# The FFN's second product with its last twelve feature blocks as a seven-product Strassen block product

## The chip, the cores and the metric

The kernel runs on one core of one Trainium2 chip. The metric is the time of the whole kernel in device microseconds (us); the median of three runs stands for a version. One more execution was taken by the hardware profiler, and all rows below come from it. Engines carry the profile's names: PE (matmul), PEld (weight load of the matmul engine), DVE (vector), ACT (scalar), POOL (GpSimd), SP (the engine that issues most transfers).

## The reference

One layer of a streaming encoder on x of 512 tokens by 1024 channels, in float32. Attention branches come first and make an intermediate x. Then the feed-forward part (FFN), of which the last product concerns us:

```python
h = rmsnorm(x, g_ffn_pre[l])
gu = h @ w_ffn_in[l]
f = (jax.nn.silu(gu[..., :D_FF]) * gu[..., D_FF:]) @ w_ffn_out[l]
x = x + rmsnorm(f, g_ffn_post[l])
```

D_FF is 2816, that is 22 feature blocks of 128; `w_ffn_out` is 2816 by 1024. So the product is 512 tokens by 2816 features by 1024 channels.

## The kernel before

Every float32 operand of a matmul is split into a high part (rounded by ACT, line 74) and a low part (the rest, subtracted by DVE, line 75), and every product is made of three matmuls: high by high, high by low, low by high. So a feature block of the second product, for one 128-token tile and one half of the channels (512 columns), is three matmuls with a 128 by 128 stationary side and 512 moving columns.

The first FFN product (`blocks`, `seven`, `left_sides`) is already a Strassen product of seven products per feature block. It leaves the gated result of feature block j in `fT[j]`, features on the partitions and 512 tokens in the columns; two neighbouring blocks share a buffer of the tag `act`.

The second product is `tok_pair` (lines 731 to 764), called with all four token tiles and `tail=4`. Its first 18 feature blocks run block by block: load the 128 by 1024 block of weights (SP, 512 KB), split it, split `fT[k]` (class `Parts`), and then for each of four token tiles six matmuls at line 745, which alternate between the two banks of that tile, 24 in all. The last four blocks (`tail`) run tile by tile and bank by bank, 24 matmuls to a tile, three in a row into one bank; when a tile is done, `done` calls `post_norm` (line 767) for it while PE goes on with the next tile. Four tiles by two halves fill all eight PSUM banks.

`post_norm` squares both halves with a sum (ACT, line 231), makes the reciprocal root (DVE line 240, POOL line 241, DVE lines 246 and 247), multiplies by the gain row (DVE, line 774), adds the residual (DVE, line 779) and stores two halves (line 781; SP and ACT queues).

Buffers: loads alternate between the tags `wraw` (3 buffers) and `lraw` (2). The split weights of alternate blocks go to `wh` and `wl` (2 each) or to `w2` (4 buffers that hold both parts). `act` has 22 buffers, `h` 8, `gate` (the scratch of `post_norm`) 2.

The order on PE is the order in which the program is written. On the other engines a planner fixes an order when the program is built: among instructions that it thinks ready it takes the one written first. On the chip each engine then runs its list in that order, and an instruction that waits holds all behind it.

Of the kernel before, what the change touches and what calls it, by code (L numbers as in the profile page):

```python
# [11 lines left out]
F32 = mybir.dt.float32  # L12
F32R = mybir.dt.float32r
AF = mybir.ActivationFunctionType
OP = mybir.AluOpType
AX = mybir.AxisListType

P = 128
T = 512
D = 1024  # L20
NK = D // P
NT = T // P
DFF = 2816
NF = DFF // P
# [23 lines left out]
class Layer:  # L48
# [41 lines left out]
    def load(self, src, kc, c, tag=None):  # L90

        self.nw += 1
        tag = tag or ("lraw" if self.late and self.nw % 2 else "wraw")
        raw = self.big(tag, F32)[:, :kc * c]
        self.nc.sync.dma_start(raw.rearrange("p (k c) -> p k c", c=c), src.rearrange("(k p) c -> p k c", p=P))
        return raw, c
# [164 lines left out]
    def run(self):  # L261
        w_in, w_kv = self.a["w_in"], self.a["w_mem_kv"]
        late = ExitStack()
        att = ExitStack()
        self.att = att.enter_context(self.tc.tile_pool(name="att", bufs=1))
        with self.tc.manual_schedule(engines={mybir.EngineType.PE}):
            self.setup()
            memT, mk, mv, cq = [], {}, {}, {}
            self.index_keys(cq)
            xs = [self.load_rows(self.a["mem"], t) for t in range(2)]  # L270
            for x in xs:
                self.norm_in(x)

            self.iq = {}
            iqs = lambda js: self.feat_tiles(w_in[:, C_IQ:C_IQ + 512], self.hT, self.iq, js, T - P, P,
                                             lambda ps: self.evac_q(ps[:, 0:T - P], T - P), self.w_iq)
            cqs = lambda js: self.feat_tiles(w_in[:, C_CQ:C_CQ + 512], self.hT, cq, js)
            mks = lambda js: self.feat_tiles(w_kv[:, 0:512], memT, mk, js, n=M)
            mvs = self.tok_tiles(w_kv[:, 512:1024], memT, (0, 1), mv)
            memTs = self.mem_T(xs, memT)  # L280
            iq = self.add(iqs(range(4)))
            kv = self.add(cqs((1,)), self.mix(memTs, cqs((2,)), 2), mks(range(4)), cqs((3,)), mvs)
            self.drain(iq)
            self.scores()
            self.drain(kv)
            a, aq = self.qkv(C_AQ, C_AK, C_AV)
            self.branch_c(cq, mk, mv)
            self.acc = {}
            self.add(self.merge(2, self.outC, "w_up_c"))
            self.drain(aq)  # L290
            self.select()
            self.fill(FM)
            b, bq = self.qkv(C_BQ, C_BK, C_BV)
            self.branch_a(*a)
            self.drain(bq)
            self.add(self.merge(0, self.outA, "w_up_a"))
            self.outB = []
            self.add(self.merge(1, self.outB, "w_up_b"))
            self.branch_b(*b)
            self.drain()  # L300
            att.close()
            self.late = late.enter_context(self.tc.tile_pool(name="late", bufs=1))
            self.mix_out()
            self.ffn()
        late.close()
# [625 lines left out]

    def ffn(self):
        nc, a = self.nc, self.a
        w_out = a["w_ffn_out"]
        fT = []

        def out(j):
            if j % 2 == 0:
                self.slot = self.big("act", F32)
            fT.append(self.slot[:, (j % 2) * T:(j % 2 + 1) * T])  # L940
            return fT[j]

        def products(pss, ws, t):
            c = slice(256 * t, 256 * t + 256)
            for ps, w in zip(pss, ws):
                yield from self.feat(ps[:, c], w, self.h2, t0=256 * t, n=256)

        run = lambda g: [None for _ in g]
        first = []
        for j, w in enumerate(self.first_ffn):  # L950
            u = (self.bank(), self.bank()), w
            run(products(*u, 0))
            first.append(u)
        pss, ws = first[0]
        for k in range(NK + 2):
            if k < NK:
                next(self.last_h2)
            if k > 1:
                for ps, w in zip(pss, ws):
                    self.feat_k(ps[:, 256:512], w, self.h2, k - 2, n=256, t0=256)  # L960
        self.gated(pss, out(0))
        y = self.right_sides()
        for j, u in enumerate(first[1:], 1):
            run(products(*u, 1))
            self.gated(u[0], out(j))
        self.blocks(range(self.NFIRST, NF), y, out)
        gp = self.grow("g_ffn_post", "h")

        def done(t, ps):
            self.post_norm(ps, gp, self.x1[t], a["out"][t * P:(t + 1) * P, :])  # L970

        self.done = done
        pairs = {}

        class Parts:
            def __getitem__(_, k):
                if k not in pairs:
                    pairs[k] = self.pair("act")
                    self.split(*pairs[k], fT[k])
                return pairs[k]  # L980

        run(self.tok_pair(w_out, Parts(), NF, range(NT), tail=4))


# [16 lines left out]
```

## Time and profile before

| what | value |
|---|---|
| median of 3 runs | 912.36 us (912.33 to 912.51) |
| the profiled execution, as a run | 910.88 us |
| its span, first to last instruction | 909.1 us |
| mean granted TensorE clock | 0.998 of full speed |
| PE busy | 888.3 us, 98% of the span |
| DVE, ACT, POOL busy | 641.5, 458.6, 117.1 us |

The busy time of an engine is the sum over all stages; what limits a stage is read from that stage's own window. A matmul's row shows its whole passage (about 0.39 us for 512 columns), of which neighbours overlap, so the pace is read from the distance between starts.

### The profile page before, as it was taken

To read this page: it belongs to the slowest core of one execution; us is meant where nothing else is said; L and a number is where in the kernel's file an instruction comes from. 1 tells how busy PE (TensorE), PEld (TensorE's weight loads), DVE (VectorE), ACT (ScalarE), POOL (GpSimd) and SP (SyncE) were. 2 spreads that over 40 slices of the span, in tenths; PEclk is the share of its full clock that TensorE was granted. 3 is DMA by queue.
4 is the path that set the end of the run, shared out by engine and by line. 5 is a ranking of instruction groups with operands and counts; after the bars stand their busy time and mean duration, and the time that the engine had idled before them with its cause. 6 is when DMAs were issued, how large, how long until landed. Compare 5 with 4: busy or idle time off the path is not lost.

```text
span 909.1 us, 13518 instructions
## 1 busy us (share of the span) xinstructions
PE 888.3 (98%) x5146; PEld 780.1 (86%) x5146; DVE 641.5 (71%) x1120; ACT 458.6 (50%) x808; POOL 117.1 (13%) x153
## 2 busy tenths in 40 slices
PE   8999999999999999999999999899999999999997
PEld 7888888888888888888788888899999999888885
DVE  6589999953688976787563478788888887932215
ACT  6465674332666665666353355455555555811111
POOL 2000000020132304433212123400000000000000
PEclk9999999999999999999999999999999999999999
DMA  6523543454354433222483624213333334533002
GB/s 203 173 83 117 168 111 93 127 128 116 104 156 112 128 82 92 70 59 58 140 252 107 185 83 127 71 47 95 115 109 102 114 97 139 164 97 106 29 1 92
DMA packets 129541, 101.17 MB, mean 111 GB/s; under 512 B 4652, under 2 KB 115292, under 8 KB 129476
## 3 DMA queue, kind: packets, MB, share of 16 engines
q1 hardware_dynamic: 128884, 99.26, 37.9%
q10 hardware_dynamic: 592, 1.05, 0.3%
q8 instruction: 40, 0.66, 0.3%
q14 instruction: 25, 0.20, 0.1%
HBM read 93.73 MB, written 2.12 MB: 105 GB/s over the span
## 4 chain that ended last, share of the span: by engine, by line
PE 82%; DVE 10%; issue 3%; ACT 2%; POOL 2%; DMA 1%; POOLq 0%; DVEq 0%; ACTq 0%
PE bank L85 19%; PE bank L86 19%; PE bank L87 19%; PE bank L745 15%; DVE wl L75 3%; PE bank L545 2%; PE bank L560 1%; PE bank L179 1%; PE bank L178 1%; PE bank L209 1%; PE bank L211 1%; PE bank L210 1%; DMA lraw<-in_w_ffn_in_dram 1%; DVE e L632 1%; POOL rs L241 1%
## 5 line engine op out<-in xcount | busy, mean ns | idle before, releaser
L75 DVE TENSOR_TENSOR wl<-wraw,wh 128x1024 fp32r<-128x1024 f32 (+1 forms) x112 | 128.5, 1149 | 101.3 <-ACT wh L74 101.0
L74 ACT CAST wh<-wraw 128x1024 fp32r<-128x1024 f32 (+1 forms) x112 | 107.2, 959 | 139.3 <-PE bank L86 74.7
L85 PE MATMUL bank<-h,wh 128*128 128x512 f32 (+1 forms) x376 | 149.0, 396 | 0.0
L87 PE MATMUL bank<-h,wl 128*128 128x512 f32 (+1 forms) x376 | 145.4, 387 | 1.0 <-DVE wl L75 0.9
L86 PE MATMUL bank<-h,wh 128*128 128x512 f32 (+1 forms) x376 | 145.1, 386 | 0.0
L745 PE MATMUL bank<-w,act 128*128 128x512 f32 x360 | 89.0, 394 | 0.0
L87 PEld LDWEIGHTS bank<-h,wl 128*128 128x128 f32 x376 | 70.6, 188 | 15.8 <-DVE wl L75 1.7
L85 PEld LDWEIGHTS bank<-h,wh 128*128 128x128 f32 x376 | 71.0, 189 | 11.6 <-issue 0.2
L86 PEld LDWEIGHTS bank<-h,wh 128*128 128x128 f32 x376 | 70.9, 188 | 11.5
L745 PEld LDWEIGHTS bank<-w,act 128*128 128x128 f32 x360 | 67.4, 188 | 14.9
L745 PE MATMUL bank<-wh,act 128*128 128x512 f32 x240 | 72.5, 393 | 0.0
L85 PE MATMUL bank<-act,wh 128*128 128x256 f32 (+1 forms) x204 | 69.3, 340 | 0.7 <-DVE s L907 0.7
L86 PE MATMUL bank<-act,wh 128*128 128x256 f32 (+1 forms) x204 | 68.0, 334 | 0.0
L87 PE MATMUL bank<-act,w 128*128 128x256 f32 x228 | 64.2, 282 | 0.0
L86 PE MATMUL bank<-act,w 128*128 128x256 f32 x228 | 64.2, 281 | 0.0
L87 PE MATMUL bank<-h,w 128*128 128x256 f32 x228 | 64.2, 281 | 0.0
L86 PE MATMUL bank<-h,w 128*128 128x256 f32 x228 | 64.2, 281 | 0.0
L85 PE MATMUL bank<-act,w 128*128 128x256 f32 x228 | 64.2, 281 | 0.0
L85 PE MATMUL bank<-h,w 128*128 128x256 f32 x228 | 64.2, 281 | 0.0
L241 POOL TENSOR_TENSOR rs<-ms,mhalf 128x1 f32<-128x1 f32 x18 | 11.6, 646 | 387.4 <-DVE ms L240 383.7
L609 POOL TENSOR_TENSOR p<-toep,score 128x128 f32<-128x128 f32 (+3 forms) x32 | 30.4, 963 | 200.2 <-DVE score L518 102.9
L745 PEld LDWEIGHTS bank<-wh,act 128*128 128x128 f32 x240 | 45.0, 188 | 9.8
(190 smaller groups left out, 2109.5 us busy)
## 6 DMA issues: line engine op xcount, KB each, us to landing
wraw<-in_w_in_dram SPq DMA_DIRECT2D x64, 512.0 KB, 3.7
lraw<-in_w_ffn_in_dram SPq DMA_DIRECT2D x22, 512.0 KB, 4.0
wraw<-in_w_ffn_in_dram SPq DMA_DIRECT2D x22, 512.0 KB, 3.7
wraw<-in_w_ffn_out_dram SPq DMA_DIRECT2D x11, 512.0 KB, 3.5
lraw<-in_w_ffn_out_dram SPq DMA_DIRECT2D x11, 512.0 KB, 3.5
wraw<-in_w_mem_kv_dram SPq DMA_DIRECT2D x8, 512.0 KB, 3.7
lraw<-in_w_out_dram SPq DMA_DIRECT2D x6, 512.0 KB, 5.5
wraw<-in_w_out_dram SPq DMA_DIRECT2D x6, 512.0 KB, 3.9
```

Of the source, the lines that this page charges most:

```text
L74: self.nc.scalar.copy(hi, src)
L75: (eng or self.nc.vector).tensor_tensor(lo, src, hi.bitcast(F32), op=OP.subtract)
L85: self.nc.tensor.matmul(out, lhsT=sh, rhs=mh, start=first and i == 0, stop=False, **kw)
L86: self.nc.tensor.matmul(out, lhsT=sh, rhs=ml, start=False, stop=False, **kw)
L87: self.nc.tensor.matmul(out, lhsT=sl, rhs=mh, start=False, stop=last and i == n - 1, **kw)
L178: self.nc.tensor.matmul(out, lhsT=x, rhs=y[:, 0:n], start=True, stop=False)
L179: self.nc.tensor.matmul(out, lhsT=x, rhs=y[:, T:T + n], start=False, stop=True)
L209: self.nc.tensor.matmul(ps, lhsT=ah[:, s], rhs=wh[:, k2], start=st, stop=False)
L241: self.nc.gpsimd.tensor_tensor(r, ms, self.mhalf, op=OP.pow)
L545: self.nc.tensor.transpose(ps[:, c:c + P], p[i][:, j * P:(j + 1) * P], self.ident)
L609: nc.gpsimd.tensor_tensor(s, toep[0][:, 0:n][:, ::-1], self.mask[i], op=OP.add)
L745: self.nc.tensor.matmul(ps[c], lhsT=st_[:, s], rhs=mv_[:, 0, c * 512:(c + 1) * 512], start=f and k == order[0], stop=l and k == order[-1])
```

## The change

The first ten feature blocks of the second product stay as they were in kind (24 matmuls per block). Their order within a token tile changes: three matmuls in a row into one bank, as in the old tail. Their weights always go to `wh` and `wl`. The last two of the ten run bank by bank, so that two banks finish first.

The last twelve blocks are cut in two halves of six feature blocks (f = 0, 1), two halves of tokens (256 each) and two halves of channels (512 each), and multiplied by a Strassen-Winograd scheme: seven products of 256 tokens by six blocks by 512 channels instead of eight, in the order 5, 1, 2, 6, 3, 7, 4. Products 1 and 2 have plain weights and plain activations; product 3 has a sum of activations, product 4 a sum of weights, and 5, 6, 7 have both. A "unit" is one product's pair of neighbouring feature blocks: three units to a product, 21 in all. The sums of activations are made by DVE (`total`). The sums of weights are made by transfers issued on POOL's queue with `accum_op` add, onto a tile that a plain load filled (`plus`): three each for products 5, 6, 7 and 4. Product 6 adds onto the tile of 5, and 4 onto that of 6, after the split of the former has read it. PSUM results are joined by ACT copies (`copied`) and DVE additions (`summed`) into SBUF, and `post_norm` reads its halves from SBUF. The first nine units are written into the plain stage, seven between its blocks and two behind it; those of 6, 3, 7, 4 are written behind products 5, 1, 2, 6.

The diff, cut to its core:

```diff
-        run(self.tok_pair(w_out, Parts(), NF, range(NT), tail=4))
+        self.ffn_out(fT)
...
+    HALF = 6
+    def ffn_out(self, fT):
...
+        room = iter(["w2"] * 4 + ["h"] * 3 + ["whl"] * 2 + ["w2"] * 4 + ["h"] * 3 + ["whl"] * 2 + ["w2"] * 3)
...
+        def plus(t, f, c, i):
+            nc.gpsimd.dma_start(two(t, 512), w_out[rows(f, i), cols[c]].rearrange("(k p) c -> p k c", p=P),
+                                accum_op=OP.add)
+            return t
...
+        def y(p, i):
+            if p == 5:
+                T[i] = plus(read(0, 0, i, "act"), 0, 1, i)
+            if p == 6:
+                plus(T[i], 1, 1, i)
+            if p == 4:
+                plus(T[i], 1, 0, i)
+            if p in (4, 5, 6):
+                return T[i]
+            if p == 7:
+                return plus(read(0, 1, i), 1, 1, i)
+            return read(*{1: (0, 0), 2: (1, 0), 3: (1, 1)}[p], i)
...
+        def prod(p, ps, first=False):
+            units = ready.pop(p)
+            for h in range(2):
+                t = slice(h * P, h * P + P)
+                for i, ((xh, xl), (wh, wl)) in enumerate(units):
+                    for k in range(2):
+                        self.passes(ps[h], [(xh[:, k, t], xl[:, k, t], wh[:, k], wl[:, k])],
+                                    first and i == k == 0, i == n - 1 and k == 1, skip_group_check=not first)
...
+        load = lambda k: self.parts(self.load(w_out[k * P:(k + 1) * P, :], 1, 1024), ("wh", "wl"))
+        for k in range(plain - 2):
+            w = load(k)
+            for t in range(NT):
+                for c in range(2):
+                    one(k, w, t, c)
+            if k and todo:
+                unit(*todo.pop(0))
...
+        prod(5, px, True)
+        s5 = copied(px)
+        summed(px, q)
+        more(6)
+        prod(1, px, True)
+        s1 = copied(px)
+        more(3)
+        prod(2, c11)
+        summed(c11, s1)
+        more(7)
+        prod(6, px)
+        summed(px, s5, OP.subtract)
+        more(4)
+        prod(3, c12)
+        summed(c12, s5)
+        out = lambda t, h0, h1: self.post_norm([h0, h1], gp, self.x1[t], self.a["out"][t * P:(t + 1) * P, :])
+        for t in range(2):
+            out(t, s1[t], s5[t])
+        prod(7, px)
+        u3 = copied(px)
+        summed(px, q, OP.subtract)
+        prod(4, c21)
+        summed(c21, u3)
+        for t in range(2):
+            out(2 + t, u3[t], q[t])
```

## Rows read from the trace of the kernel before

**Rows 1.** The page's head: span, then busy time, share and instructions of each engine
```profile
span 909.1 us, 13518 instructions
...
PE 888.3 (98%) x5146; PEld 780.1 (86%) x5146; DVE 641.5 (71%) x1120; ACT 458.6 (50%) x808; POOL 117.1 (13%) x153
```

**Rows 2.** The page's chain that ended last, by engine
```profile
PE 82%; DVE 10%; issue 3%; ACT 2%; POOL 2%; DMA 1%; POOLq 0%; DVEq 0%; ACTq 0%
```

**Rows 3.** Windows: first 18 blocks, tail of four, end; busy us, granted clock, DMA share
```profile
core 0: us, PE busy (x) PEld busy (x) DVE busy (x) ACT busy (x) POOL busy (x), PEclk, DMA share, GB/s
780.87:879.87 99.00, 99.00 (x435) 81.19 (x434) 33.42 (x37) 26.39 (x33) 0.00 (x0) 1.00 0.26 79
879.87:902.35 22.48, 22.48 (x97) 17.85 (x95) 10.58 (x22) 4.81 (x14) 1.65 (x3) 1.00 0.19 71
902.35:909.10 6.75, 0.01 (x1) 0.00 (x0) 2.60 (x6) 0.69 (x2) 0.55 (x1) 0.76 0.20 78
```

**Rows 4.** Timeline of PE, second product: start us, busy us, what
```profile
780.87 0.63 PE L745 MATMUL bank<-wh,act 128*128 128x512 f32 x2
...
786.33 5.67 PE L745 MATMUL bank<-w,act 128*128 128x512 f32 x24
791.84 0.40 PE L745 MATMUL bank<-wh,act 128*128 128x512 f32 x1
...
879.84 0.40 PE L745 MATMUL bank<-wh,act 128*128 128x512 f32 x1
...
901.49 0.86 PE L745 MATMUL bank<-w,act 128*128 128x512 f32 x3
```

**Rows 5.** Who waited for whom, 779 us to the end: us, times, longest
```profile
POOL rs L241 <- DVE ms L240: 317.6, 4, 302.4
...
PE bank L85 <- DVE s L907: 0.7, 1, 0.7
```

**Rows 6.** Groups by line and shape, 765 us to the end: busy us, mean ns
```profile
L75 DVE TENSOR_TENSOR act<-act 128x512 fp32r<-128x512 f32 x22 | 13.8, 685 | 0.0
L75 DVE TENSOR_TENSOR w<-lraw,w 128x1024 fp32r<-128x1024 f32 x11 | 13.5, 1224 | 25.8 <-ACT w L74 25.7
...
L74 ACT CAST act<-act 128x512 fp32r<-128x512 f32 x22 | 12.3, 617 | 2.8 <-DVE act L75 2.7
L74 ACT CAST wh<-wraw 128x1024 fp32r<-128x1024 f32 x11 | 11.6, 1053 | 38.9 <-PE bank L745 38.9
...
L774 DVE SCALAR_TENSOR_TENSOR prod<-bank,h 128x512 f32<-128x512 f32 x8 | 5.5, 686 | 7.2 <-ACT junk L231 7.2
L231 ACT ACTIVATE junk<-bank 128x512 f32<-128x512 f32 x8 | 4.8, 598 | 22.1 <-PE bank L745 15.4 <-DVE fin L779 6.7
```

**Rows 7.** Transfers: where to and from, queue, count, KB each, us to landing
```profile
lraw<-in_w_ffn_out_dram SPq DMA_DIRECT2D x11, 512.0 KB, 3.5
...
lraw<-in_w_out_dram SPq DMA_DIRECT2D x6, 512.0 KB, 5.5
...
act<-act SPq DMA_DIRECT2D x9, 256.0 KB, 3.7
```

**Rows 8.** Timeline of all engines at the start of the second product
```profile
775.96 1.04 ACT L74 CAST wh<-wraw 128x1024 fp32r<-128x1024 f32 x1
...
777.72 1.22 DVE L75 TENSOR_TENSOR wl<-wraw,wh 128x1024 fp32r<-128x1024 f32 x1
```

**Rows 9.** Timeline of all engines behind the last matmul
```profile
902.46 0.60 ACT L231 ACTIVATE junk<-bank 128x512 f32<-128x512 f32 x1 [1.99 <-PE bank L745]
...
903.18 0.21 DVE L240 TENSOR_SCALAR ms<-ss 128x1 f32<-128x1 f32 x1 [1.99 <-ACT junk L231]
...
903.47 0.55 POOL L241 TENSOR_TENSOR rs<-ms,mhalf 128x1 f32<-128x1 f32 x1 [5.04 <-DVE ms L240]
...
904.50 1.42 DVE L779 SCALAR_TENSOR_TENSOR fin<-prod,rs,fin 128x512 f32<-128x512 f32 x2
905.95 0.34 ACTq L781 DMA_DIRECT2D out_dram<-fin  x1
```

More of the change, by code (lines that the diff above doesn't have):

```diff
@@ L933, in ffn @@
         nc, a = self.nc, self.a
-        w_out = a["w_ffn_out"]
         fT = []
@@ L939, in out @@
                 self.slot = self.big("act", F32)
-            fT.append(self.slot[:, (j % 2) * T:(j % 2 + 1) * T])
-            return fT[j]
+            fT.append(self.slot)
+            return self.slot[:, (j % 2) * T:(j % 2 + 1) * T]
         def products(pss, ws, t):
@@ L966, in ffn @@
         self.blocks(range(self.NFIRST, NF), y, out)
+        self.ffn_out(fT)
+    HALF = 6
+    def ffn_out(self, fT):
+        nc, w_out = self.nc, self.a["w_ffn_out"]
         gp = self.grow("g_ffn_post", "h")
[L969 to L980, printed above, removed]
@@ L982, in ffn, with rows @@
-        run(self.tok_pair(w_out, Parts(), NF, range(NT), tail=4))
+        plain = NF - 2 * self.HALF
+        n = self.HALF // 2
+        cols = slice(0, 512), slice(512, 1024)
+        bank = [[self.bank() for _ in range(2)] for _ in range(NT)]
+        room = iter(["w2"] * 4 + ["h"] * 3 + ["whl"] * 2 + ["w2"] * 4 + ["h"] * 3 + ["whl"] * 2 + ["w2"] * 3)
+        two = lambda t, c: t.rearrange("p (k c) -> p k c", c=c)
+        def rows(f, i):
+            k = plain + f * self.HALF + 2 * i
+            return slice(k * P, (k + 2) * P)
@@ new lines, in read @@
+        def read(f, c, i, tag=None):
+            return self.load(w_out[rows(f, i), cols[c]], 2, 512, tag)[0]
+        def plus(t, f, c, i):
+            nc.gpsimd.dma_start(two(t, 512), w_out[rows(f, i), cols[c]].rearrange("(k p) c -> p k c", p=P),
+                                accum_op=OP.add)
+            return t
+        T = {}
+        def y(p, i):
[10 more added lines that the diff above has]
+            return read(*{1: (0, 0), 2: (1, 0), 3: (1, 1)}[p], i)
@@ new lines, in right, with left, total @@
+        def right(p, i):
+            src, r = y(p, i), next(room)
+            if r == "w2":
+                t = self.wide()
+                hi, lo = t[:, 0:1024], t[:, 1024:2048]
+            else:
+                hi, lo = (self.big(x) for x in (("h", "h") if r == "h" else ("wh", "wl")))
+            self.split(hi, lo, src)
+            return two(hi, 512), two(lo, 512)
+        S = {}
+        def left(p, i):
+            f1, f2 = (two(fT[plain + f * self.HALF + 2 * i], 512) for f in range(2))
+            x11, x12, x21, x22 = f1[:, :, 0:256], f2[:, :, 0:256], f1[:, :, 256:512], f2[:, :, 256:512]
+            def total(a, b, op, to=None):
+                if to is None:
+                    if i % 2 == 0:
+                        S[p] = self.big("act", F32)
+                    to = two(S[p][:, (i % 2) * 512:(i % 2) * 512 + 512], 256)
+                nc.vector.tensor_tensor(to, a, b, op=op)
+                return to
+            if p == 5:
+                S[0, i] = total(x21, x22, OP.subtract)
+            if p == 6:
+                total(S[0, i], x11, OP.subtract, S[0, i])
+            if p == 3:
+                total(S[0, i], x12, OP.add, S[0, i])
+            x = S[0, i] if p in (3, 5, 6) else total(x11, x21, OP.subtract) if p == 7 else {1: x11, 2: x12, 4: x22}[p]
+            t = self.big("act")
+            hi, lo = two(t[:, 0:512], 256), two(t[:, 512:1024], 256)
+            self.split(hi, lo, x)
+            return hi, lo
@@ new lines, in unit @@
+        def unit(p, i):
+            ready.setdefault(p, []).append((left(p, i), right(p, i)))
+        def prod(p, ps, first=False):
[6 more added lines that the diff above has]
+                                    first and i == k == 0, i == n - 1 and k == 1, skip_group_check=not first)
@@ new lines, in ffn_out, with act, one @@
+        ready, pairs = {}, {}
+        todo = [(p, i) for p in (5, 1, 2) for i in range(n)]
+        def act(k):
+            if k not in pairs:
+                pairs[k] = self.pair("act")
+                self.split(*pairs[k], fT[k][:, (k % 2) * 512:(k % 2) * 512 + 512])
+            return pairs[k]
+        def one(k, w, t, c):
+            a, s = act(k), slice(t * P, (t + 1) * P)
+            self.passes(bank[t][c], [(a[0][:, s], a[1][:, s], w[0][:, 0, cols[c]], w[1][:, 0, cols[c]])],
+                        k == 0, k == plain - 1)
@@ new lines, in ffn_out @@
+        load = lambda k: self.parts(self.load(w_out[k * P:(k + 1) * P, :], 1, 1024), ("wh", "wl"))
[6 more added lines that the diff above has]
+                unit(*todo.pop(0))
+        ws = {k: load(k) for k in (plain - 2, plain - 1)}
+        order = [(2, 1), (3, 1), (0, 0), (1, 0), (0, 1), (1, 1), (2, 0), (3, 0)]
+        px = bank[2][1], bank[3][1]
@@ new lines, in ffn_out, with copied @@
+        half = lambda t: (t[:, 0:512], t[:, 512:1024])
+        q = half(self.big("act", F32))
+        for t, c in order:
+            for k, w in ws.items():
+                one(k, w, t, c)
+            if (t, c) == (3, 1):
+                for x, ps in zip(q, px):
+                    nc.scalar.copy(x, ps)
+        for u in todo:
+            unit(*u)
+        more = lambda p: [unit(p, i) for i in range(n)]
+        def copied(ps):
+            out = half(self.big("act", F32))
+            for x, y_ in zip(out, ps):
+                nc.scalar.copy(x, y_)
+            return out
@@ new lines, in summed @@
+        def summed(ps, s, op=OP.add):
+            for x, y_ in zip(s, ps):
+                if op == OP.add:
+                    nc.vector.tensor_tensor(x, y_, x, op=op)
+                else:
+                    nc.vector.tensor_tensor(x, x, y_, op=op)
+            return s
+        c11, c12, c21 = ((bank[t][c], bank[t + 1][c]) for t, c in ((0, 0), (0, 1), (2, 0)))
+        prod(5, px, True)
[4 more added lines that the diff above has]
+        s1 = copied(px)
```

## The prediction

> **What bounds the kernel now.** First the page's head: PE is busy for 98% of the span, the next engine, DVE, for 71% [rows 1]. A share can mislead where stages differ, so next comes the chain that ended last: 82% of it is PE [rows 2]. Then the windows of the stage that is changed. The second product's first 18 blocks take 99 us in which PE is busy throughout at full clock, while DVE works 33 us, ACT 26 and POOL not at all; its last four blocks take 22.5 us, again with PE busy throughout; behind them lie 6.75 us without matmuls [rows 3]. Last, the waits from 779 us on: PE waited once, 0.7 us, just ahead of the second product, and POOL lay idle for over 300 us [rows 5]. So this stage is PE and a closing chain. A removed matmul shortens it by its pace, as long as the side work keeps out of PE's way.
>
> **The matmuls: a gain of 6.8 us.** The old product issues 22 blocks x 24 = 528 matmuls of 512 columns. The new one issues 10 x 24 = 240 for the plain blocks and, to each product, 2 token tiles x 6 blocks x 3 passes = 36, seven times: 252. That is 492, or 36 fewer. The pace has two values. In the first 18 blocks, where matmuls alternate between two banks, a block takes 791.84 - 786.33 = 5.51 us, and all 18 take 879.84 - 780.87 = 98.97 us, 0.229 us to a matmul. In the tail, three in a row into one bank, the 94th matmul of 96 starts 901.49 - 879.84 = 21.65 us after the first, 0.233 us to a matmul [rows 4]. The new code issues everything in the tail's order, so I price all 492 at 0.2328. Before: 98.97 + 96 x 0.2328 = 121.3 us. After: 492 x 0.2328 = 114.5 us. Naively 36 x 0.2328 would be 8.4; the slower order of 432 matmuls takes 1.6 back. At the old pace of 0.229 everywhere the stage would take 112.8 us, 8.5 fewer; that is the good bound.
>
> **Where PE would then be.** From 780.9: plain blocks to 836.8; each product is 8.4 us, so product 5 ends at 845.2, 1 at 853.6, 2 at 862.0, 6 at 870.4, 3 at 878.7, 7 at 887.1, 4 at 895.5.
>
> **The side work on DVE and ACT: nothing, hidden by PE.** A weight split of 1024 columns costs ACT 1.05 and DVE 1.22 us, an activation split or sum of 512 columns ACT 0.62 and DVE 0.69 [rows 6]. A unit then costs DVE 1.9 us, 2.6 with a sum of activations, and ACT 1.7. Plain stage, 56 us long: DVE 10 x 1.9 for the blocks, 7 x 1.9 and 3 x 0.7 for the units in it, 34 us. In the products, the tightest load on DVE is that of products 6 and 7: three units with sums, 7.8, and one joining of two banks, 1.4, is 9.2 us against 8.4 us of PE. That would bind if it lasted, but it doesn't: work for 6 may begin when product 5 has given up its buffers at 845.2 and is needed at 862.0. Run in order, 6 is ready by 854.4, 3 by 862.2 (needed 870.4), 7 by 871.4 (needed 878.7), 4 (5.7 and 1.4) by 878.5 (needed 887.1). Some 7 to 8 us of cover remain for each. Without it each late us would be a us of PE. ACT has 3 x 1.7 and two copies of 0.6, 6.2 us, to a product. A bank that a later product overwrites (`px`) is evacuated half by half while PE works for 4.2 us on the other half; the evacuation costs DVE and ACT 0.7 each. The sums of `out` for the first two token tiles fall under products 7 and 4.
>
> **The start: 0.4 us, between 0 and 2.** Weights had six places (`wh`, `w2`) and now two. The first block's split lay on ACT at 775.96 and on DVE from 777.72 to 778.94, 1.9 us before PE began [rows 4, 8]; that cover is thin. Later, a place is free when the block before last ends, so the split (2.3 us) has one block, 5.6 us, to be done: 3.3 us of slack, into which one unit (2.6 us of DVE) just fits if it stands ahead. A wait of ACT or DVE inside a unit can eat that slack; SP, too, issues in order, and a load that waits for its buffer holds the loads behind it.
>
> **The adding transfers: nothing, between nothing and 12 us.** The trace of before has none, nor any transfer from POOL. Nearest rows: a plain load of 512 KB of these weights lands 3.5 us after its issue, the worst-placed kind takes 5.5, and a copy of 256 KB from SBUF to SBUF takes 3.7 [rows 7]. An adding transfer reads the weights and reads and writes the tile: from 3.5 (the add rides along) to 3.5 + 2 x 3.7 = 10.9 us (the tile's 512 KB as a copy of its own). I take 6, nearer to the load, which it resembles. None can gain: the plain loads stay. Deadlines: for product 5, plain load and adding need 10 us at 6, 14 at 10.9, and product 5 begins 56 us into the stage; for 6 the adding waits for 5's splits only; for 4 the tiles are free once 6 is split, at 854.4, three in a row at 10.9 are done by 887.1, exactly when PE wants product 4, at 6 by 872.4. POOL's only other work here, four tiny powers, is behind. Every adding waits on POOL for the plain load or the last reader of its tile, and holds POOL's queue, which nobody else needs then.
>
> The Trainium skill says (SBUF — State Buffer, "Who interferes with whom") that GpSimd builds the descriptors of its transfers through a port pair that VectorE can hold shut in its two-port modes, and that the transfer then starves. It also says that `tensor_tensor`, nearly all of DVE's work here, has no such mode; by that, nothing is added to the sum, and lateness from this cause is less likely. No run here shows it. The skill's fit for GpSimd transfers (DMA: Bandwidth & Descriptors, "Anatomy of one DMA — SWDGE (gpsimd) path"), 2.0 us and 436 GB/s, makes my estimate 3.2 us for 512 KB, and 5.6 us if three streams are charged; the sum would be the same by it.
>
> **The end: 1.2 us lost, between 0.7 and 2.2.** Before, 902.46 to 905.95 is a chain for one tile: square on ACT, DVE, POOL's power, DVE, last store; the span ends at 909.1 [rows 3, 9]. Now the last bank must first be added into SBUF by DVE: 0.69 and a hand-over of about 0.1. And the last two token tiles share the end: the third tile's bank is finished 18 x 0.233 = 4.2 us ahead of the fourth's, while its own chain, with the sum (0.7) and then 902.46 to 905.9, takes 4.2 and some; so its last two DVE operations (1.42 us) can stand in front of the last sum. I take 0.4 for that, with ends at 0 and 1.4.
>
> **The sum.** -6.8 + 0.4 + 0 + 1.2 = -5.2 us. The profiled execution is a run of 910.88 us, whose span is 909.1; the median is 912.36, 1.5 us more. I apply the difference to the median: 907.2 us.
>
> **Rivals.**
> 1. *The adding transfers come late and PE waits* (slower). Place: the plain stage. The three units of product 5 stand in ACT's list among the splits of blocks 2 to 4; if the list was made for a short adding and it takes long, ACT waits at the unit's weight copy and the next block's split behind it is late. Price: 10.9 - 3.5 = 7.4 us of lateness, less 3.3 us of slack, 4.1 us for each of three units, 12.3 us: 919.5 us; with one third of that, 911.3. It decides the sign from 5.2 us of waiting on, that is when an adding takes about 5 us longer than the list allows. For it: a thin two-place buffer and an operation that no row prices. Against: those units have 40 us until PE needs them, and a list that sets them late costs nothing. Chance 0.14.
> 2. *The gain is mostly lost to small waits* at the start (2 us), at a product that waits for a DVE list in a poor order (1 us), and at the end (2.2): -6.8 + 5.2 = -1.6, 910.8 us. For it: 9.2 us of DVE work to 8.4 of PE in two of the products, and a DVE list fixed ahead of time. Against: 7 us of cover. Chance 0.18.
> 3. *PE keeps the old pace* of 0.229, since the two orders differ for another reason than the bank: -8.5 + 0.8 = -7.7, 904.7 us. Against: the tail's order is the new one instruction for instruction. Chance 0.08.
>
> **How the numbers follow.** The forecast (905.2 to 909.2) has 0.60. About 0.2%, 1.8 us, is what a measurement of this kernel can tell from no change, so faster means below 910.5 and slower above 914.2. Faster: forecast 0.60, rival 3 0.08, half of rival 2 0.09, nothing of rival 1: 0.77. Same: the other half of rival 2, 0.09, and a little of rival 1, 0.03. Slower: the rest of rival 1, 0.11. The range goes from 904.6, the old pace, to 912.0, which takes in rival 2 whole, and leaves out about 0.15 on the slow side and 0.03 on the fast.
>
> **What would show it.** Right: 492 matmuls of the second product at 0.233 us; PE without gaps from its first matmul to about 895; the group of sums (line of `total`, `summed`) at 0.69 us; adding transfers that land 4 to 8 us after issue; some 7.9 us behind the last matmul. Wrong: waits of PE for `wl` or for right sides named in the waits; ACT or DVE idle with a transfer as releaser between 785 and 815 us (rival 1); a gap of PE at the start of product 6, 7 or 4 (rival 2); a pace of 0.229 (rival 3); a granted clock that falls behind a gap, which would make any wait dearer.

## The result and the profile after

The changed kernel takes 932.94 us (median of 4 runs, 932.16 to 933.91) against 912.40 for the kernel before on the same chips: a ratio of 1.0228, 95% interval 1.0216 to 1.0241. It is 20.5 us slower. The forecast was 907.2, with a range to 912.0.

The page's head answers to [rows 1]: PE's share falls from 98% to 96% with 36 matmuls fewer, so PE must now be waiting.

```profile
span 930.4 us, 13563 instructions
...
PE 889.2 (96%) x5110; PEld 779.0 (84%) x5110; DVE 671.6 (72%) x1162; ACT 476.6 (51%) x834; POOL 133.7 (14%) x165
```

The windows of the second product show where, as in [rows 3]. I cut at the first matmul, at PE's gaps and at the last matmul.

```profile
core 0: us, PE busy (x) PEld busy (x) DVE busy (x) ACT busy (x) POOL busy (x), PEclk, DMA share, GB/s
782.48:793.40 10.92, 10.92 (x50) 8.83 (x48) 4.56 (x7) 3.27 (x5) 1.96 (x2) 1.00 0.78 234
793.40:814.89 21.49, 9.88 (x28) 6.88 (x28) 9.54 (x10) 6.89 (x8) 4.06 (x4) 0.73 0.66 134
814.89:843.50 28.61, 28.61 (x122) 23.29 (x120) 11.61 (x14) 10.59 (x14) 1.22 (x1) 0.96 0.57 157
843.50:845.64 2.14, 0.92 (x4) 0.48 (x3) 1.23 (x1) 0.48 (x1) 0.00 (x0) 1.00 0.01 6
845.64:892.00 46.36, 46.36 (x204) 38.04 (x203) 22.87 (x29) 17.27 (x26) 7.30 (x6) 1.00 0.53 104
892.00:919.40 27.40, 24.36 (x94) 19.12 (x92) 19.87 (x33) 11.50 (x21) 1.96 (x3) 0.88 0.20 56
919.40:930.40 11.00, 0.00 (x0) 0.00 (x0) 6.02 (x13) 1.33 (x4) 1.75 (x2) 0.66 0.25 95
```

Three stretches have PE idle: 793 to 815, around 844, and one after 892. In the first and the last of them the mean granted clock is 0.73 and 0.88 of full speed. Behind the last matmul 11.0 us pass, where 6.75 did [rows 3]. PE's waits from 775 us on (in total, times, longest), where before there was one of 0.7 us [rows 5]:

```profile
PE bank L85 <- ACT wh L74: 10.5, 3, 7.0
PE bank L85 <- DVE act L1111: 3.0, 1, 3.0
PE bank L86 <- DVE wl L75: 2.4, 3, 0.9
PE bank L85 <- DVE s L907: 2.3, 1, 2.3
```

PE waits for ACT's split of a plain block (`wh`). What did ACT wait for? Its timeline, with the idle time and its releaser in brackets:

```profile
792.33 1.05 ACT L74 CAST w<-act 128x1024 fp32r<-128x1024 f32 x1 [7.03 <-DMA act<-in_w_ffn_out_dram]
793.29 1.04 ACT L74 CAST h<-wraw 128x1024 fp32r<-128x1024 f32 x1
798.48 1.04 ACT L74 CAST w<-act 128x1024 fp32r<-128x1024 f32 x1 [4.15 <-DMA act<-in_w_ffn_out_dram]
799.43 1.04 ACT L74 CAST wh<-lraw 128x1024 fp32r<-128x1024 f32 x1
800.37 0.61 ACT L74 CAST act<-act 128x512 fp32r<-128x512 f32 x1
810.80 1.04 ACT L74 CAST w<-act 128x1024 fp32r<-128x1024 f32 x1 [9.81 <-DMA act<-in_w_ffn_out_dram]
...
895.09 1.05 ACT L74 CAST wh<-lraw 128x1024 fp32r<-128x1024 f32 x1 [14.22 <-DMA lraw<-in_w_ffn_out_dram]
```

`w<-act` is product 5's weight sum. ACT stands 7.0, 4.2 and 9.8 us for its three adding transfers, and the next plain block's split, `wh<-lraw` at 799.43, stands behind the second. PE had been without work since 793.5. At 895.09 the same happens for a sum of product 7 (its second: of its three additions two go onto `wraw` tiles, and the middle one onto this `lraw`). POOL's own timeline shows why they are late:

```profile
782.25 1.37 POOL L996 DMA_DIRECT2D act<-in_w_ffn_out_dram  x1 [198.04 <-DVE act L908]
792.57 1.23 POOL L996 DMA_DIRECT2D act<-in_w_ffn_out_dram  x1 [8.96 <-DMA act<-in_w_ffn_out_dram]
798.71 1.21 POOL L996 DMA_DIRECT2D act<-in_w_ffn_out_dram  x1 [4.91 <-issue]
804.84 1.23 POOL L996 DMA_DIRECT2D act<-in_w_ffn_out_dram  x1 [4.91 <-issue]
...
876.95 1.22 POOL L996 DMA_DIRECT2D act<-in_w_ffn_out_dram  x1 [5.04 <-ACT act L74]
883.02 1.21 POOL L996 DMA_DIRECT2D act<-in_w_ffn_out_dram  x1 [4.85 <-issue]
889.09 1.22 POOL L996 DMA_DIRECT2D lraw<-in_w_ffn_out_dram  x1 [4.85 <-issue]
```

They go one at a time. From 792.57 on those that follow each other directly are 6.1 us apart, and between them POOL waits 4.9 us for nothing that another engine does ("issue"). From issue to landing they take (shortest, median, longest):

```profile
DMA to landing us min/median/max: 5.7/5.9/10.1
```

The longest is the first: issued at 782.25, it is waited for by ACT until 792.33, in the window in which the DMA engines are 78% busy. And the third, at 798.71, is not product 5's: it is product 6's first, onto the first tile of product 5, the only one whose split was done by then (DVE's part of the second's starts at 799.55). Product 5's third leaves at 804.84, one place later, and ACT goes on at 810.80. At the end the addition for product 7 is the last of the twelve, behind all three of product 4, which is needed later. Transfers from 765 us to the end by queue (packets, MB, share of 16 engines), and the adding ones (KB each, median us to landing):

```profile
q0 software_dynamic: 3264, 6.29, 24.2%
q1 hardware_dynamic: 5679, 13.11, 23.3%
...
act<-in_w_ffn_out_dram POOLq DMA_DIRECT2D x9, 512.0 KB, 5.9
```

6.3 MB of adding transfers (q0) hold the DMA engines as long as 13.1 MB of plain ones (q1).

The balance, from the starts in PE's timeline: the first matmul of the stage is 782.48 - 780.87 = 1.6 us later; from there to the last one's end 136.9 us pass in place of 121.5, so +15.4; behind it +4.3. That is +21.3 us, the difference of the two spans. Within the 136.9 us, 492 matmuls would need 112.4 (measured without gaps in the last experiment but one), so 24.5 us are gaps and half clock: 16.7 between 793 and 817, 1.8 at 844, 3.1 and 2.9 from 896.5 to 906. The half clock is seen in the distance between starts in PE's timeline, 0.43 us; the granted clock is 0.50 from 802 to 805 us:

```profile
800.52 0.80 PE L85 MATMUL bank<-wh,act 128*128 128x512 f32 x1 [6.97 <-ACT wh L74]
...
802.99 0.63 PE L85 MATMUL bank<-wh,act 128*128 128x512 f32 x1
803.41 0.63 PE L86 MATMUL bank<-wl,act 128*128 128x512 f32 x1
```

### The profile page after: what moved, and what is told of

Same layout as the page of the kernel before. It is cut to its first block, busy times and chain, and to the rows that moved or that the text cites. A ratio compares the mean times of both kernels' runs of the same rounds, so it can differ in the third digit from the quotient of the medians.

```text
span 930.4 us, 13563 instructions
## 1 busy us (share of the span) xinstructions
PE 889.2 (96%) x5110; PEld 779.0 (84%) x5110; DVE 671.6 (72%) x1162; ACT 476.6 (51%) x834; POOL 133.7 (14%) x165
## 3 DMA queue, kind: packets, MB, share of 16 engines
q0 software_dynamic: 3264, 6.29, 4.3%
## 4 chain that ended last, share of the span: by engine, by line
PE 73%; DVE 11%; issue 8%; DMA 3%; POOL 2%; ACT 2%; POOLq 0%; DVEq 0%; ACTq 0%
PE bank L86 20%; PE bank L85 20%; PE bank L87 20%; DVE wl L75 3%; PE bank L745 3%; PE bank L545 2%; PE bank L560 1%; PE bank L179 1%; PE bank L178 1%; DVE act L75 1%; PE bank L209 1%; PE bank L211 1%; PE bank L210 1%; DMA wraw<-in_w_ffn_out_dram 1%; DVE e L632 1%
## 5 line engine op out<-in xcount | busy, mean ns | idle before, releaser
L75 DVE TENSOR_TENSOR wl<-wraw,wh 128x1024 fp32r<-128x1024 f32 (+1 forms) x105 | 119.9, 1143 | 67.9 <-ACT wh L74 67.6
L74 ACT CAST wh<-wraw 128x1024 fp32r<-128x1024 f32 (+1 forms) x105 | 99.9, 953 | 104.1 <-PE bank L86 74.9
L86 PEld LDWEIGHTS bank<-h,wh 128*128 128x128 f32 x376 | 70.8, 188 | 11.5
L85 PE MATMUL bank<-h,act 128*128 128x256 f32 (+2 forms) x152 | 47.4, 312 | 3.0 <-DVE act L1111 3.0
L85 PE MATMUL bank<-wh,act 128*128 128x512 f32 x96 | 40.0, 417 | 10.5 <-ACT wh L74 10.5
L86 PE MATMUL bank<-h,act 128*128 128x256 f32 (+2 forms) x152 | 46.2, 304 | 1.1 <-DVE h L79 1.1
L75 DVE TENSOR_TENSOR w<-wl,w 128x1024 fp32r<-128x1024 f32 x38 | 46.2, 1216 | 1.0 <-ACT w L74 0.6
L87 PE MATMUL bank<-act,wl 128*128 128x512 f32 (+1 forms) x128 | 46.5, 364 | 0.0
```

Source lines behind the costliest of these rows:

```text
L74: self.nc.scalar.copy(hi, src)
L75: (eng or self.nc.vector).tensor_tensor(lo, src, hi.bitcast(F32), op=OP.subtract)
L85: self.nc.tensor.matmul(out, lhsT=sh, rhs=mh, start=first and i == 0, stop=False, **kw)
L86: self.nc.tensor.matmul(out, lhsT=sh, rhs=ml, start=False, stop=False, **kw)
L87: self.nc.tensor.matmul(out, lhsT=sl, rhs=mh, start=False, stop=last and i == n - 1, **kw)
```

## The experiments

The stretch ahead of the second product ends later in some profiled executions than in others: PE comes to its last wait ahead of the stage at 778.3 to 778.6 us in four of them and at 780.0 to 781.5 in the rest, and already the last POOL addition of line 839 starts at 582.1 to 582.5 us in the same four and at 583.6 to 584.8 in the rest. These runs don't show what sets this. So I compare two lengths inside the stage: "stage" is from its first matmul to the end of its last, "end" is what is behind that. Both are from one profiled execution of each kernel. The first five edits were run once; 25 runs of the kernel before lay between 911.0 and 915.0 us on one chip, so a us or two in the time of a single run says nothing.

| kernel | time, us | kernel before, same chip | stage | end |
|---|---|---|---|---|
| before | 912.4 | | 121.5 | 6.75 |
| changed | 932.9 | 912.4 | 136.9 | 11.0 |
| no additions | 911.1 | 912.1 | 115.7 | 9.4 |
| plain transfers from POOL | 913.6 | 912.1 | 115.5 | 9.4 |
| scratch doubled | 922.8 | 912.1 | 126.8 | 9.7 |
| 5's additions ahead | 926.0 | 912.1 | 129.1 | 12.2 |
| 5's sums by DVE | 921.1 | 912.7 | 125.0 | 11.5 |
| all sums by DVE | 909.8 | 912.7 | 114.7 | 9.5 |
| all by DVE, gain row later | 910.2 | 912.7 | 115.1 | 9.5 |
| the same, early halves ahead | 910.6 | 912.7 | 116.2 | 9.6 |
| sums of 5 and 7 by DVE | 909.9 | 912.2 | 115.8 | 9.6 |
| all by DVE, blocks 8 and 9 reordered | 906.0 | 912.2 | 112.4 | 9.6 |
| 5 and 7 by DVE, reordered, early halves | 907.6 | 912.2 | 115.7 | 9.2 |

An edit can also change the lists that the planner makes for ACT, DVE and POOL elsewhere in the stage; where that mattered it is said. The diffs are cut ("...").

**No additions.** The transfers are left out, all else stays.

```diff
         def plus(t, f, c, i):
-            nc.gpsimd.dma_start(two(t, 512), ..., accum_op=OP.add)
             return t
```

> The twelve adding transfers are left out, so the right sides of products 5, 6, 7 and 4 lack the added blocks of weights. Theory (the adding transfers come one at a time, about 6.1 us apart, and the lists of ACT and DVE are held at their results): PE runs without gaps over 1 us from its first matmul of the second product, 492 x 0.228 = 112 us, and the run takes 904 to 908 us. Rival (the seven-product form itself is too tight: two places for plain weights, DVE's work per product): the gaps of the plain stage stay, and the run stays above 920 us.

Measured: 911.1 us, 21.8 under the changed kernel; PE's wait of 10.5 us is down to 0.5, and that of 3.0 is gone. PE's waits in this kernel:

```profile
PE bank L85 <- DVE s L907: 2.5, 1, 2.5
PE bank L86 <- DVE wl L75: 0.8, 1, 0.8
PE bank L85 <- ACT wh L74: 0.5, 1, 0.5
```

So the additions cost more than the whole loss. But 911.1 is not the 904 to 908 expected: the new form without them gains 1 us at most, which one run can't tell from nothing. The stage is 5.8 us shorter than before; against that the end takes 9.4 us, not 7.9, a wait of 2.5 us stands at the start, and 1.2 us are waited where the plain stage ends.

**Plain transfers from POOL.** The same transfers without `accum_op`.

> The twelve transfers on POOL's queue stay, with the same bytes and waits, but as plain loads that overwrite the tile (so products 5, 6, 7 and 4 use one block where a sum belongs). If the addition is what makes them slow: they land in 3.5 to 4.5 us, follow each other at under 5 us, and the run takes 912 to 922 us. If any transfer from POOL's queue comes one at a time with a long landing: landing 5 to 6 us, distance about 6 us, and the run stays within 3 us of the 932 of the changed kernel.

Measured: 913.6 us; landing 4.9 us in the median (4.0 to 8.0), between the two expectations, and issues 1.2 to 1.9 us apart where nothing else held them:

```profile
854.48 0.72 POOL L996 DMA_DIRECT2D act<-in_w_ffn_out_dram  x1
856.41 0.72 POOL L996 DMA_DIRECT2D act<-in_w_ffn_out_dram  x1 [1.20 <-issue]
```

That is 2.5 us more than without transfers, but PE came to its last wait ahead of the stage 1.3 us later, and stage and end are as long as there (115.5 and 9.4 us); one wait of 0.9 us, at 804 us, is new. So POOL's queue alone costs about 1 us of the 21.8, and the rest is the addition. Its transfers are issued slower (1.2 us, not 0.7), land later and, with this scratch, go one at a time. They also hold the DMA engines twice as long, in nearly twice as many packets: here the twelve transfers take

```profile
q0 software_dynamic: 1728, 6.29, 11.9%
```

where the adding ones were 3264 packets and 24.2%.

**Scratch doubled.**

```diff
-    nc = bacc.Bacc("TRN2", ..., dynamic_dma_scratch_size=1024)
+    nc = bacc.Bacc("TRN2", ..., dynamic_dma_scratch_size=2048)
...
-        ... bufs=1 + (n == "s3")) for n in ("s1", "s2", "s3"))
+        ... bufs=1) for n in ("s1", "s2", "s3"))
```

> The descriptor scratch of POOL's transfers doubled to 2048 bytes per partition; to make room, one scratch tile of the first product (s3) has 1 buffer in place of 2. If POOL waits 4.9 us between transfers because the scratch holds the descriptors of only one: neighbouring transfers that wait for nothing else are issued 1 to 3.5 us apart in place of 6.1, and the run gains 3 to 10 us. If the next one waits for the landing of the former for another reason: 6.1 us stays, and the run is within 3 us of 932.

Measured: 922.8 us, 10.1 gained. Two transfers now leave back to back, in POOL's timeline:

```profile
796.25 2.46 POOL L996 DMA_DIRECT2D act<-in_w_ffn_out_dram  x2 [8.61 <-DVE w L75]
799.80 1.21 POOL L996 DMA_DIRECT2D act<-in_w_ffn_out_dram  x1 [1.09 <-DVE w L75]
```

and most land later (DMA issues: KB each, median us from issue to landing):

```profile
act<-in_w_ffn_out_dram POOLq DMA_DIRECT2D x9, 512.0 KB, 9.5
```

So the 4.9 us of waiting were for room in the scratch, which held one adding transfer. With two in flight the median landing goes from 5.9 to 9.5 us, 4.75 us per transfer; that they then wait for each other in the DMA engines is my reading. ACT still stands 6.3, 1.5 and 8.9 us at product 5's sums, and the lists stay as they were.

**Product 5's additions ahead.** Its loads and transfers are written before the plain stage, its units behind those of product 1.

```diff
...
-        todo = [(p, i) for p in (5, 1, 2) for i in range(n)]
+        todo = [(p, i) for p in (1, 5, 2) for i in range(n)]
+        early = {(5, i): y(5, i) for i in range(n)}
```

> Loads and additions for product 5 are written ahead of the plain stage, and the units of product 1 ahead of those of 5, each unit with the buffers it had. Theory (the list of ACT stands still at a weight sum while the next plain block's split is behind it): the gaps of 7 and 7 us in the plain stage shrink to under 3 us together, the late sum of product 7 stays, and the run takes 912 to 922 us. Rival (the transfers themselves are too slow wherever they stand): the gaps move but stay over 10 us together, and the run is above 926 us.

Measured: 926.0 us, where the rival begins, but with 7 us of gaps in the plain stage, between the two expectations. Of the plain stage's two long waits one is left, 5.8 us; the second addition left POOL only 8.6 us after the first, and ACT stood 8.1 us for it. The profile names DVE's split of an activation as what released it, but ACT goes on with the first sum at 788.71, and the second addition leaves at 788.95: once more just behind the landing of the one before it. So the room in the scratch still set their pace. The late sum of product 7 stayed: PE waits 2.7 us for line 1114, the subtraction at product 6.

**Product 5's sums by DVE.**

```diff
-                T[i] = plus(read(0, 0, i, "act"), 0, 1, i)
+                T[i] = read(0, 0, i, "act")
+                nc.vector.tensor_tensor(T[i], T[i], read(0, 1, i), op=OP.add)
```

> Product 5's three sums of weights are made by DVE (both blocks loaded by SP, one addition of 128x1024 each); the other nine stay adding transfers. Theory (the stall of the plain stage is ACT's list standing at product 5's adding transfers): PE's gaps between 790 and 820 us and the half clock behind them go, some 16 us, and the run takes 914 to 919 us, with the late sum of product 7 left. Rival (the plain stage stalls because all adding transfers and loads share the DMA engines): gaps over 5 us stay there, and the run is above 923 us.

Measured: 921.1 us, 11.8 gained. No single wait of PE between 790 and 820 us is over 1 us now: the plain stage's stall was ACT's list at product 5's additions. It missed the 914 to 919 expected because the sum of product 7, still last of nine on POOL, now holds PE for 5.7 us in place of 3.0. ACT's waits (total, times, longest):

```profile
ACT wh L74 <- DMA lraw<-in_w_ffn_out_dram: 18.2, 2, 18.1
```

and PE's:

```profile
PE bank L85 <- DVE act L1112: 5.7, 1, 5.7
```

DVE's list holds the low part of that split ahead of the subtraction that reads product 6 out of its banks (line 1112 here, 1111 in the changed kernel), so product 7 cannot begin, though its first units are ready.

**All sums by DVE.** `plus` loads the second block by SP and adds it by DVE.

```diff
-            nc.gpsimd.dma_start(two(t, 512), ..., accum_op=OP.add)
+            nc.vector.tensor_tensor(t, t, read(f, c, i), op=OP.add)
```

> All twelve sums of weights by DVE, none by an adding transfer. DVE gets 12 x 1.2 = 14.7 us more. Theory (DVE has that room, 76 us of work in 115 before): within 2 us of the kernel without any additions (911.1), so 909 to 913 us. Rival (DVE binds in the products, where it had 9.2 us of work to 8.4 of PE): PE waits for right sides of products 6, 7 or 4, 3 us or more in sum, and the run takes over 914 us.

Measured: 909.8 us, ratio 0.9968 (0.9955 to 0.9981) to the kernel before, and no wait of PE at a product. DVE had the room: it is 77 to 100% busy between 840 and 890 us, and PE waits for none of it. Left are 1.8 us of waits at 827 us, where the plain stage ends.

**Gain row later.** The load of 512 KB at the start of `ffn_out` moves behind the plain stage.

> As the former, and the load of the gain row (512 KB) is written behind the plain stage in place of ahead of it. Theory (at the start ACT stands at a weight split of product 1 whose load shares the DMA engines with the gain row; block 21's evacuation behind it is late, PE waits 2.5 us and its clock falls): the wait falls below 1 us, the run gains 1.5 to 4 us against the former. Rival (ACT would stand there anyway, as the list puts these splits early): under 0.8 us.

Measured: 910.2 us, stage 115.1 and 114.7 without the edit: nothing. But the run does not decide between the two expectations: with the sums on DVE the lists had already changed at the start, and PE's wait there was 1.1 us in both, so the wait of 2.5 us was not there to be removed. It was 2.3 to 2.6 us in the changed kernel and the first three edits and 0.9 to 1.1 in the others, whose lists differ; what sets it is not settled.

**Early halves ahead.** For the last two token tiles the half that is ready before product 4 is squared and multiplied early.

> As the former, and for the last two token tiles the squares and gain products of the half that is ready early are written ahead of product 4, in place in SBUF. The time behind the last matmul, 9.4 us without the additions, falls to 7.3 to 8.2 us and the run gains 1.2 to 2.1 us against the former. If the closing chain is bound elsewhere (stores, POOL): under 0.6 us.

Measured: 910.6 us, an end of 9.6 us: nothing. On DVE the third tile's last two operations still stand ahead of the fourth tile's sum, which waits 1.8 us:

```profile
900.56 1.42 DVE L1155 SCALAR_TENSOR_TENSOR fin<-act,rs,fin 128x512 f32<-128x512 f32 x2
901.89 0.68 DVE L1108 TENSOR_TENSOR act<-bank,act 128x512 f32<-128x512 f32 x1
```

**Sums of 5 and 7 by DVE,** those of 6 and 4 by adding transfers.

> Sums of weights for products 5 and 7 by DVE, those for 6 and 4 stay adding transfers: six in place of twelve, all with a deadline some 20 us or more behind the moment from which they can run. Theory (an adding transfer costs nothing where the lists leave it that time): within 2 us of the kernel with all sums by DVE (909.8), no wait of PE at a right side of products 6, 7 or 4. Rival (any adding transfer in the stage costs time, through POOL's one-at-a-time issue or the DMA engines): 914 us or more.

Measured: 909.9 us, ratio 0.9973 (0.9963 to 0.9984), the same as with all on DVE. Six adding transfers, landing in 7.0 us in the median (5.8 to 10.6), cost no wait at a product, as expected where the lists leave them their time. The stage is 1.1 us longer; a plain block waits 0.95 us at 809 us.

**Blocks 8 and 9 reordered.** All sums by DVE; the last two plain blocks run over four banks with block 8, then with 9.

```diff
...
-        for t, c in order:
-            for k, w in ws.items():
-                one(k, w, t, c)
+        for t, c, k in [(*order[j], k) for b in (range(4), range(4, 8)) for k in ws for j in b]:
+            one(k, ws[k], t, c)
```

> All sums by DVE, and the last two plain blocks run over four banks with the first block, then with the second, in place of both blocks bank by bank. Theory (both blocks' weights are needed at once, but the second's place comes free only as block 7 ends, so PE waits 1.9 us for a split of 2.3 us, whatever makes the sums): that wait goes, and the run gains 1 to 2.5 us against the kernel with all sums by DVE, 907 to 909 us. Rival (the wait only moves to the later banks or to product 5): under 0.6 us.

Measured: 906.0 us, ratio 0.9930 (0.9917 to 0.9943), the fastest of all: 6.2 us under the kernel before on that chip. PE waits for nothing in the stage:

```profile
782.58:895.00 112.42, 112.42 (x494) 92.10 (x492) 85.08 (x108) 52.57 (x75) 2.78 (x3) 1.00 0.46 154
895.00:904.60 9.60, 0.01 (x1) 0.00 (x0) 5.07 (x10) 1.33 (x4) 0.93 (x1) 0.63 0.28 109
```

492 matmuls in 112.4 us are 0.2285 us each. It gained 2.3 us of stage for a wait of 1.8 and a slow matmul beside it; the mechanism expected for it holds, though the median is under the 907 to 909 us expected.

**5 and 7 by DVE, reordered, early halves.**

> Sums for 5 and 7 by DVE, for 6 and 4 by adding transfers, the order of the last two plain blocks changed, and the early halves of the last two token tiles squared and multiplied ahead. Theory: the parts add up, 905 to 908 us; the time behind the last matmul falls from 9.5 to 8 to 8.6 us, as DVE is not behind when the last product ends. Rival (the closing chain stays at 9.5 us since the third tile's last operations still stand ahead of the fourth's sum): 908 to 910 us.

Measured: 907.6 us, ratio 0.9947 (0.9935 to 0.9959). The parts did not add up: the wait between blocks 8 and 9 is gone, but two blocks ahead of it, at 803 and 810 us, wait 0.9 and 1.6 us, and the end is 9.2 us, since the third tile's operations again stand ahead of the fourth's sum.

## Why the prediction was wrong

*The step that failed* is the term "The adding transfers: nothing". As the prediction put it, they take 6 us, product 5's need 10 to 14 us of the 56 before PE wants them, and a queue that nobody else needs may wait. The landing was right in the median, 5.9 us, though the first took 10.1. The estimate of 5.6 us, worked out from the Trainium skill (DMA: Bandwidth & Descriptors, "Anatomy of one DMA — SWDGE (gpsimd) path") with three streams charged, was near that median as well. What the deadline missed is that PE is not the first to wait. ACT meets the sum where the planner put it in its list, and behind it stands the split of a plain block that PE wants within 5.5 us. Taking the additions out gained 21.8 us; taking out product 5's alone gained 11.8. That they were 40 us early for PE helped nothing.

*Three things made it dearer than rival 1 allowed* (at most 919.5). It was the right mechanism at the right place, but priced as if each landing came by itself. First, the scratch held one transfer, so neighbours came 6.1 us apart; a larger one gained 10 us. I had three in a row at 10.9 us in the bound, but only for product 4. Second, the clock: after the gap of 7.0 us the next matmuls start 0.43 us apart, at 1.2 GHz, and so again after 814.3 and after 899.9; some 31 matmuls at that pace, 0.2 us each, are 6 to 7 us. Third, POOL's order, which I had down as harmless: product 6's first addition stood ahead of product 5's third and made it 6.1 us later, and product 7's stood behind product 4's, and through DVE's list held the reading of product 6, 3.1 us and a clock fall. No run changed POOL's order alone, so its share is not shown by itself.

*The matmuls* were better than forecast: 112.4 us against 114.5. Three in a row into one bank did not keep the old tail's 0.2328; the pace was 0.2285. The 9.1 us saved is the good bound, 8.5, and a little more. So rival 3, with a chance of 0.08, had the pace right; its sum adds 0.8 us where the forecast's own start and end give 1.6. Why the old tail was slower these runs don't show.

*The side work on DVE and ACT* was hidden, as said: even with 14.7 us more on DVE no product waited. *The start*, 0.4 us forecast, cost 1.6 in the changed kernel and, by PE's wait of 1.1 us in place of 0.7, 0.4 with all sums by DVE. The thin cover was named, the place was not: the end of the plain stage, where two blocks are needed at once from two places, cost 1.8 to 2.5 us, slow matmuls included, in the versions that keep the old order there (in one of them, early halves ahead, more slow matmuls follow).

*The end* was forecast at +1.2 us, at most +2.2. It is +2.9 in the fastest version and +4.3 in the changed kernel, where DVE was behind. The sum in front (0.7) was right; that the third tile's operations stand ahead of the last sum was named but put at 0.4, and it is 1.1 us in the fastest version and 2.7 in the changed kernel; POOL's power was 0.4 longer, and the ready half's square was not done ahead.

*The sum without the additions* would still have been off: with them left out the run takes 911.1 us, with all sums by DVE 909.8, near rival 2's 910.8. What rival 2 says is what happened there, though at the start, the end of the plain stage and the end, and not at a product. Only with the reordering is the size near: -9.1 for the matmuls and +2.9 for the end are -6.2, and the fastest version gains 6.2. That the two agree to a tenth is luck, as the profiled execution of that version lost another 1.7 us ahead of its first matmul.

## What to carry to other kernels

A result's deadline is set by the first engine whose list it stands in, not by the engine that consumes it: for each new transfer, find what is queued behind its reader. An operation that no row prices should be tested for how many can be in flight, not only for how long one takes. And a gap of PE costs more than its length when the clock falls behind it.

## What was not expected of the hardware

An adding transfer of 512 KB from HBM to SBUF landed 5.9 us after its issue in the median with one in flight, 9.5 with two; the plain one from the same queue took 4.9, from SP 3.9. It held the DMA engines twice as long as the plain one from the same queue (24.2% against 11.9% for 6.3 MB), in 272 packets against 144, and about twice as long per byte as SP's loads (23.3% for 13.1 MB).

POOL's reciprocal power on 128 x 1, untouched by the change, went from 0.55 us [rows 9] to 0.93, in every version I looked at, also with all sums by DVE, where POOL issues none of the additions. In POOL's timeline of the kernel without additions:

```profile
881.17 0.93 POOL L241 TENSOR_TENSOR rs<-ms,mhalf 128x1 f32<-128x1 f32 x1 [295.63 <-DVE ms L240]
```

What runs beside it on DVE is the gain product, which now reads both operands from SBUF and before read one from PSUM. The Trainium skill (SBUF — State Buffer, "Who interferes with whom") says that a DVE instruction with two SBUF inputs contends with a GpSimd one that reads SBUF; these rows agree, though no run changed that operand alone.
